# One load with a repeating source for the attention operands, and the neighbourhood bias loaded one block ahead

## The chip, the cores and the metric

The kernel runs on one core of one Trainium2 chip. The metric is the device time of one execution in microseconds, as the median of several runs. The engines are TensorE (PE, with its weight loads PEld), VectorE (DVE), ScalarE (ACT), GpSimd (POOL) and SyncE (SP). SP and POOL issue the DMAs here.

## What is computed

One inference step of a two-layer backbone, for 128 context tokens (the prompt) and 512 latent tokens, 640 columns in all, with model width 1024. Each layer normalises its input, sends it through one input projection into four parallel token mixers, merges them with sigmoid gates, projects, and adds a SwiGLU FFN:

```python
    A gated DeltaNet, bidirectional, chunked, centred short conv on q/k/v;
    B differential attention with learned lambda and 2-D axial rotary on latent tokens;
    C HGRN2 gated linear recurrence with state expansion, bidirectional, chunked;
    D 2-D neighbourhood attention (min(8,ROWS) x 16 window, relative-position bias).
```

The change concerns mixers B and D. In both, latent queries see 256 cached context keys and their own keys; in D a latent query sees a window of the 8 x 64 grid, and a relative-position bias is added to its scores, masked outside the window:

```python
        p = jax.nn.softmax(jnp.einsum('bhqmd,bhkmd->bhmqk', qi, k).astype(F32) * scale, axis=-1)
        pd = p[:, :, 0] - lam * p[:, :, 1]
```

## The kernel before

Everything is float32 in value. A product of two float32 operands is made of three float32r products, high x high, high x low and low x high (`unit`, L294), so weights and activations are split into a rounded high part on ACT (`whi`, `hh`) and a rest on VectorE and POOL (`wlo`, `hl`). Weights stream from DRAM through two raw buffers `wraw`, issued on SP.

Inside a layer, `weave` (L173) interleaves Python generators and thereby fixes the order of PE's instructions by hand. The chains are the mixers' serial parts (`mix_a`, `mix_b`, `mix_c`, `mix_d`, `prep_a`, `prep_b`), the fill is the long projections (`store_fm`, `store_tok`, `pregate`, `merge`), whose product is the PSUM tile `pu`. A chain's step names what it waits for in `yield`; the planner holds a time for each tile, for a DMA the moment of its issue plus `DLAT` = 2300 ns whatever its shape, and puts the step before the next piece of fill once that time has passed. The order of ACT, VectorE, POOL and SP comes from the tile framework's scheduler. An engine works through its queue in order, so an instruction that waits holds up what stands behind it.

Mixer D (`mix_d`, L1373) has four pairs of heads in each layer, eight turns in all, called heads below. At the start of each it loads the prompt's operands, the latent queries of block 0 (`dqt`), the latent keys (`dkd`, two tiles with high and low parts in opposite halves of the partitions) and, in `split_ctx` (L1082), the raw context keys, twice, into the upper and lower 64 partitions of the tile `dod`; ACT casts them to `dkc` and VectorE forms the rests. `dod` is also the head's output tile: it comes from a pool of four buffers, and the store `oT<-dod` of the head before returns one. Then the prompt's own attention follows (scores `pds`, exponentials `dP`, transposes, products `pdo`), then four blocks of 128 latent queries. A block loads its bias `dbias` (L1451), yields until that and the rest are there, makes the scores `pds`, adds the bias on VectorE, takes the exponentials `dPl`, transposes them (`pdt`) and multiplies by the values. `dqt` of a block is loaded while the block before is worked on; `dbias` is loaded at its own block. All of D's loads are issued on SP.

Mixer B (`mix_b`, L1160) has four heads in each layer, with rotary queries and keys prepared by `prep_b` (L1051), which writes high and low parts to the DRAM tiles `bqk`. `mix_b` loads `bqt` (queries of 128 tokens, both copies of 64 rows) and `bKd` from there, on POOL, and the context keys through the same `split_ctx`, on SP, into `bo`, with the cast `bKc`. POOL also computes a part of `wlo`.

## Time and profile before

| | us |
|---|---|
| median of 3 runs | 3498.42 (3497.09 to 3504.01) |
| the profiled execution | 3495.77 |
| its span, first to last instruction | 3493.8 |
| PE busy in it | 3366.3 |
| DVE / ACT / POOL busy | 2366.3 / 1427.7 / 544.1 |

The mean granted clock of TensorE is 0.985 of full speed. Mixer D's context keys are loaded at 668 us for its first head and at 2704 us for its last. To read the tables: a wait is idle time of an engine, put down to what ended it; the chain follows the last instruction of a stretch back to what released it; a tile's view lists what its writers and readers waited for. Matmuls overlap with their weight loads, and a busy PE is not a PE at its peak.

### The profile page before, as it was taken

What the parts mean: (1) busy time and instruction counts of PE and PEld (TensorE: products, weight loads), DVE (VectorE), ACT (ScalarE), POOL (GpSimd) and SP (SyncE); (2) the same over time, 40 slices, a digit from 0 to 9 for tenths busy, and PEclk for the clock granted to TensorE, in tenths of its full rate; (3) what the DMA queues carried; (4) which work ended last, traced back from release to release, by engine and by line L of the source; (5) the groups of instructions that cost most, each with busy time, mean ns of one, the idle gap of its engine ahead of it and who ended that gap; (6) DMA issues with size and microseconds to landing.
All of it is one profiled execution on the core that took longest, in us unless ns stands there. A gap on an engine that the chain in (4) does not pass through costs nothing.

```text
span 3493.8 us, 63676 instructions
## 1 busy us (share of the span) xinstructions
PE 3366.3 (96%) x23932; PEld 3294.3 (94%) x23932; DVE 2366.3 (68%) x5497; ACT 1427.7 (41%) x3170; POOL 544.1 (16%) x592
## 2 busy tenths in 40 slices
PE   8999999899999999999999999999999999999998
PEld 5998999899999999999999899999999999999998
DVE  7689888865667577887456797778555656644445
ACT  5344444544453353222243455445444433522222
POOL 2221112421122100000002212124122121000000
PEclk9999999999999999999999999999999999999999
DMA  6444334865453354554244433348454334322222
GB/s 218 151 151 140 120 104 136 239 177 164 121 153 120 116 173 134 153 152 128 81 123 147 132 111 116 102 127 245 141 145 125 89 103 159 108 67 78 76 78 67
DMA packets 297931, 460.16 MB, mean 132 GB/s; under 512 B 48148, under 2 KB 193172, under 8 KB 297624
## 3 DMA queue, kind: packets, MB, share of 16 engines
q1 hardware_dynamic: 286296, 423.58, 39.3%
q0 software_dynamic: 11328, 32.52, 3.1%
q8 instruction: 189, 3.10, 0.4%
q14 instruction: 118, 0.97, 0.1%
HBM read 368.42 MB, written 87.56 MB: 131 GB/s over the span
## 4 chain that ended last, share of the span: by engine, by line
PE 69%; DVE 6%; DMA 5%; issue 3%; ACT 2%; POOL 1%; SPq 0%; DVEq 0%; ACTq 0%; POOLq 0%
PE pu L152 54%; PE ptk L152 2%; PE pdv L152 1%; PE pbs L152 1%; PE pbo L152 1%; PE pW L152 1%; PE pX L152 1%; PE pdt L158 1%; PE pT L152 1%; PE pca L152 1%; PE pds L152 1%; DVE cacc L107 1%; DMA wraw<-in_wd 1%; DVE wlo L107 1%; DMA moT<-oT 1%
## 5 line engine op out<-in xcount | busy, mean ns | idle before, releaser
L152 PE MATMUL pu<-hh,whi 128*128 128x320 f32 (+1 forms) x3760 | 1195.8, 318 | 18.1 <-ACT stg L107 14.9
L152 PE MATMUL pu<-hl,whi 128*128 128x320 f32 (+1 forms) x3760 | 1166.9, 310 | 2.4 <-DVE hl L107 2.4
L152 PE MATMUL pu<-hh,wlo 128*128 128x320 f32 (+1 forms) x3760 | 1167.3, 311 | 0.0
L152 PEld LDWEIGHTS pu<-hh,whi 128*128 128x128 f32 (+1 forms) x3760 | 709.2, 189 | 22.6 <-ACT stg L107 15.4
L152 PEld LDWEIGHTS pu<-hl,whi 128*128 128x128 f32 (+1 forms) x3760 | 709.5, 189 | 4.5 <-DVE hl L107 2.6
L152 PEld LDWEIGHTS pu<-hh,wlo 128*128 128x128 f32 (+1 forms) x3760 | 708.0, 188 | 1.7
L107 ACT CAST whi<-wraw 128x1024 fp32r<-128x1024 f32 (+2 forms) x410 | 390.5, 953 | 653.6 <-PE pu L152 422.7
L107 POOL TENSOR_TENSOR wlo<-wraw,whi 128x416 fp32r<-128x416 f32 (+1 forms) x209 | 324.5, 1554 | 1757.3 <-ACT whi L107 1509.9
L107 DVE TENSOR_TENSOR wlo<-wraw,whi 128x608 fp32r<-128x608 f32 (+3 forms) x410 | 389.7, 951 | 260.6 <-ACT whi L107 256.9
L152 PE MATMUL pu<-fa,whi 128*128 128x320 f32 x1152 | 253.6, 309 | 0.0
L152 PE MATMUL pu<-mo,whi 128*128 128x320 f32 x1024 | 235.1, 317 | 5.2 <-DVE mo L107 3.5
L107 DVE SCALAR_TENSOR_TENSOR x<-pu,gn,x 128x128 f32<-128x128 f32 (+1 forms) x336 | 136.6, 436 | 88.8 <-PE pu L152 87.1
L152 PEld LDWEIGHTS pu<-fa,whi 128*128 128x128 f32 x1152 | 192.6, 188 | 0.0
L152 PE MATMUL ptk<-whi,hh 128*128 128x256 f32 x640 | 192.1, 300 | 0.0
L498 DVE CUSTOM_DVE_ANT_0 junk<-wa,cs,mod 128x256 bf16<-128x256 f32 (+1 forms) x288 | 171.7, 596 | 24.9 <-DMA wa<-in_wada 20.8
L152 PE MATMUL ptk<-wlo,hh 128*128 128x256 f32 x640 | 182.0, 284 | 3.2 <-DVE wlo L107 3.2
L152 PE MATMUL ptk<-whi,hl 128*128 128x256 f32 x640 | 181.9, 284 | 0.0
L152 PEld LDWEIGHTS pu<-mo,whi 128*128 128x128 f32 x1024 | 173.0, 191 | 7.5 <-DVE mo L107 4.8
L152 PE MATMUL pu<-fa,wlo 128*128 128x320 f32 x576 | 177.8, 309 | 0.0
L152 PE MATMUL pu<-mo,wlo 128*128 128x320 f32 x512 | 160.0, 313 | 0.0
L152 PEld LDWEIGHTS ptk<-wlo,hh 128*128 128x128 f32 x640 | 123.4, 193 | 3.4 <-DVE wlo L107 3.4
L152 PEld LDWEIGHTS ptk<-whi,hh 128*128 128x128 f32 x640 | 123.7, 193 | 0.0
(422 smaller groups left out, 6123.9 us busy)
## 6 DMA issues: line engine op xcount, KB each, us to landing
wraw<-in_win SPq DMA_DIRECT2D x151, 512.0 KB, 3.8
wa<-in_wada SPq DMA_DIRECT2D x116, 256.0 KB, 3.0
wraw<-in_wg SPq DMA_DIRECT2D x44, 512.0 KB, 3.4
wraw<-in_wu SPq DMA_DIRECT2D x44, 512.0 KB, 3.5
wraw<-in_wd SPq DMA_DIRECT2D x80, 256.0 KB, 2.6
p<-stg SPq DMA_DIRECT2D x112, 160.0 KB, 2.8
wa<-in_wada SPq DMA_DIRECT2D x128, 128.0 KB, 2.4
wraw<-in_wtok SPq DMA_DIRECT2D x32, 512.0 KB, 3.9
```

The source lines that it names most:

```text
L107: r = f(*args, **kw)
L152: r = self.nc.tensor.matmul(out, lhsT, rhs, start=start, stop=stop)
L158: r = self.nc.tensor.transpose(out, src, ident)
L498: self.nc.vector.tensor_tensor_reduce(junk, raw, cs[g], 0.5, o if k0 else self.bada[:, l, m:m + 1], ALU.mult, ALU.add, o)
```

## The change

Three things are done.

1. The operands of B's queries and of D's keys get DRAM layouts of their own. `bqk` is parted into `bq` (64 rows of four blocks of 512 floats: for each 128 tokens high and low parts side by side) and `bk`; the keys of `dqk` move to `dkk`, with 256 rows in the order in which the two tiles `dkd` take them. One load of `bqt` replaces two, and one of `dkd` replaces two (of 64 rows), that is two a head instead of four. `prep_b` stores B's queries in four pieces instead of three.
2. `twice` builds a source pattern that names the same 64 rows two times, with a step of 0 in front. With it `bqt` and the raw context keys in `split_ctx` (`dod` and `bo`) are one load of 128 rows instead of two of 64.
3. `biases(b)` loads the bias; it is called for block 0 at block 0, and for block b + 1 in block b, behind the queries of block b + 1.

The whole diff:

```diff
--- before.py
+++ after.py
@@ -92,6 +92,16 @@
         p, c = i
         n = c.start // self.w
         return self.parts[n][p, c.start - n * self.w:c.stop - n * self.w]
+
+
+def dr(ap, off, *dims):
+
+    return bass.AP(tensor=ap.tensor, offset=ap.offset + off, ap=[list(d) for d in dims])
+
+
+def twice(ap, off, *dims):
+
+    return dr(ap, off, (0, 2), *dims)
 
 
 class Timed:
@@ -324,7 +334,7 @@
                     a.mul(t[:, :c0], ps[:, :c0], f)
                     self.dma(self.pd[m][:, :c0], t[:, :c0])
                 hi, lo = self.GS("sth", HT - c0, F32R), t[:, c0:].bitcast(F32R)
-                out = self.dqk[m % 4][int(f)]
+                out = self.dqk[m % 4] if f < 1 else self.dkk[m % 4]
                 if f < 1:
                     a.mul(t[:, c0:].rearrange("p (b r c) -> p r b c", b=4, c=16), ps[:, c0:HT].rearrange("p (r b c) -> p r b c", b=4, c=16), f)
                 else:
@@ -334,7 +344,8 @@
                     if f < 1:
                         self.dma(out[i].rearrange("p (b x) -> p b x", b=4)[:, :, 16 * r.start:16 * r.stop], x.rearrange("p (b x) -> p b x", b=4))
                     else:
-                        self.dma(out[i, :, 64 * r.start:64 * r.stop], x)
+
+                        self.dma(dr(out, (0, 64)[i] * TL + 64 * r.start, ((192, 64)[i] * TL, 2), (TL, 64), (1, 64 * (r.stop - r.start))), x)
             else:
                 a.copy(t, ps[:, :HT])
                 self.dma(self.pd[m][:, j * HT:(j + 1) * HT], t)
@@ -1072,18 +1083,19 @@
             self.a.copy(hi, x)
             v.tensor_tensor(lo, x, r, ALU.subtract)
 
-            for i in range(2):
-                d = self.bqk[h][i]
-                self.dma(d[:64], r[:64, i], QB)
-                self.dma(d[192:], r[64:, i], QB)
-                self.dma(d[64:192], x[:, i], QB)
-            self.ev[('b', h)] = self.t[self.bqk[h].tensor.name]
+
+            q, d = self.bq[h], self.bk[h]
+            for b, src in enumerate((r[:64, 0], x[:64, 0], x[64:, 0], r[64:, 0])):
+                self.dma(dr(q, b * 128, (4 * TL, 64), (512, 4), (1, 128)), src.rearrange("p (t c) -> p t c", c=128), QB)
+            self.dma(d[:64], r[:64, 1], QB)
+            self.dma(d[192:], r[64:, 1], QB)
+            self.dma(d[64:192], x[:, 1], QB)
+            self.ev[('b', h)] = self.t[d.tensor.name]
 
     def split_ctx(self, kc, tmp, src):
 
         raw = tmp[:, :512]
-        self.dma(raw[:64], src)
-        self.dma(raw[64:], src)
+        self.dma(raw, twice(src, 0, (512, 64), (1, 512)))
         for m in range(2):
             o_ = slice(64 - m * 64, 128 - m * 64)
             c = raw[:, m * 256:m * 256 + 256]
@@ -1175,14 +1187,12 @@
 
             Kd, Kc = [self.SA("bKd", dt=F32R) for _ in range(2)], self.SA("bKc", dt=F32R)
             Kc = [Kc[:, 0:256], Kc[:, 256:512]]
-            dq, dk = self.bqk[h][0], self.bqk[h][1]
+            dq, dk = self.bq[h], self.bk[h]
 
             def queries(t):
 
                 x = self.SA("bqt", dt=F32R)
-                src = dq[:, t * 128 - 128:t * 128].rearrange("(b p) c -> p b c", b=4)
-                for i in range(2):
-                    self.dma(x[i * 64:i * 64 + 64].bitcast(F32).rearrange("p (b c) -> p b c", b=4), src, QM)
+                self.dma(x.bitcast(F32), twice(dq, t * 512 - 512, (4 * TL, 64), (1, 512)), QM)
                 return x
             qt = {1: queries(1)}
             for m in range(2):
@@ -1388,7 +1398,7 @@
             kd, kc = [self.SA("dkd", dt=F32R) for _ in range(2)], self.SA("dkc", dt=F32R)
             kc = [kc[:, 0:256], kc[:, 256:512]]
             od = self.S("dod")
-            dq, dk = self.dqk[hp][0], self.dqk[hp][1]
+            dq, dk = self.dqk[hp], self.dkk[hp]
 
             def queries(b):
 
@@ -1397,10 +1407,13 @@
                 for i in range(2):
                     self.dma(x[i * 64:i * 64 + 64].bitcast(F32).rearrange("p (b c) -> p b c", b=4), src, QD)
                 return x
+            def biases(b):
+                x = self.SA("dbias").rearrange("p (h k) -> p h k", h=2)[:, :, :8 * WIN[b][1]]
+                self.dma(x, self.I['nab'][l, 2 * hp:2 * hp + 2, :, BOFF[b]:BOFF[b] + 8 * WIN[b][1]].rearrange("h p k -> p h k"), QD)
+                return x
             qt = {0: queries(0)}
             for hh in range(2):
-                for i in range(2):
-                    self.dma(kd[hh][i * 64:i * 64 + 64].bitcast(F32), dk[i ^ hh, hh * 64:hh * 64 + 64], QD)
+                self.dma(kd[hh].bitcast(F32), dk[128 * hh:128 * hh + 128], QD)
             self.split_ctx(kc, od, self.I['ckd'][l, hp])
 
             yield q, pr, vf
@@ -1447,11 +1460,12 @@
                     a.copy(vo, vi)
                 else:
                     self.g.tensor_scalar(vo, vi, 1.0, None, ALU.mult)
-                bias = self.SA("dbias").rearrange("p (h k) -> p h k", h=2)[:, :, :nk]
-                self.dma(bias, self.I['nab'][l, 2 * hp:2 * hp + 2, :, BOFF[b]:BOFF[b] + nk].rearrange("h p k -> p h k"))
+                if b == 0:
+                    bias = {0: biases(0)}
                 if b < 3:
                     qt[b + 1] = queries(b + 1)
-                yield bias, qt[b], kd[1], kc[1]
+                    bias[b + 1] = biases(b + 1)
+                yield bias[b], qt[b], kd[1], kc[1]
                 Ps, rcs = [], []
                 pss = []
                 for hh in range(2):
@@ -1467,7 +1481,7 @@
                     mc, ml = self.sm("d_mc", 1), self.sm("d_ml", 1)
                     nm, ss, rc = self.sm("d_nm", 1), self.sm("d_ss", 1), self.sm("d_rc", 1)
                     v.tensor_reduce(mc, ps[:, :256], AX.X, ALU.max)
-                    v.tensor_tensor_reduce(ps[:, 256:256 + nk], ps[:, 256:256 + nk], bias[:, hh], 1.0, mc, ALU.add, ALU.max, ml)
+                    v.tensor_tensor_reduce(ps[:, 256:256 + nk], ps[:, 256:256 + nk], bias[b][:, hh], 1.0, mc, ALU.add, ALU.max, ml)
                     v.tensor_scalar(nm, ml, -1.0, None, ALU.mult)
                     P = self.SA("dPl")
                     a.activation(P[:, :256 + nk], ps[:, :256 + nk], ACT.Exp, bias=nm, accum_out=ss)
@@ -1667,8 +1681,10 @@
                 t = self.pd['qk', h] = self.dr.tile([2, 128, T], F32, tag=f"qk{h}", name=f"qk{h}")
                 self.pd[16 + h], self.pd[20 + h] = t[0], t[1]
 
-            self.dqk = [self.dr.tile([2, 2, 128, TL], F32, tag=f"dqk{h}", name=f"dqk{h}") for h in range(4)]
-            self.bqk = [self.dr.tile([2, 256, TL], F32, tag=f"bqk{h}", name=f"bqk{h}") for h in range(4)]
+            self.dqk = [self.dr.tile([2, 128, TL], F32, tag=f"dqk{h}", name=f"dqk{h}") for h in range(4)]
+            self.dkk = [self.dr.tile([256, TL], F32, tag=f"dkk{h}", name=f"dkk{h}") for h in range(4)]
+            self.bq = [self.dr.tile([64, 4 * TL], F32, tag=f"bq{h}", name=f"bq{h}") for h in range(4)]
+            self.bk = [self.dr.tile([256, TL], F32, tag=f"bk{h}", name=f"bk{h}") for h in range(4)]
             self.ad = [self.dr.tile([4, 128, T], F32, tag=f"ad{i}", name=f"ad{i}") for i in range(4)]
             self.pg = P(name="pg", bufs=3, space=PSUM)
             self.pm = P(name="pm", bufs=5, space=PSUM)
```

The planner's rules are as they were, but a block of D no longer yields to a bias that was issued at that moment, and this moves the order of PE. The place is the end of block 0 in the first head (`pdv<-cst,do` transposes the block's output, `pds` are the scores of block 1, `pbo` and `pbs` are mixer B's, `pu` is fill). Before, PE went on with twelve products `pu` after that transpose, and then:

```order
L152 MATMUL pbo<-bv,be 128x128
L152 MATMUL pbs<-bKd,bqt 128x512 x2
L152 MATMUL pbs<-bKc,bqt 128x256 x2
L152 MATMUL pu<-hh,whi 128x320
L152 MATMUL pu<-hl,whi 128x320
L152 MATMUL pu<-hh,wlo 128x320
L152 MATMUL pds<-dkc,dqt 128x256 x2
```

With the change, the scores follow the transpose at once:

```order
L168 MATMUL pdv<-cst_127,do 128x128
L162 MATMUL pds<-dkc,dqt 128x256 x2
L162 MATMUL pds<-dkd,dqt 128x256 x2
L162 MATMUL pds<-dkc,dqt 128x256 x2
L162 MATMUL pds<-dkd,dqt 128x256 x2
L162 MATMUL pu<-hh,whi 128x320
```

So the score products of block 1 stand 20 instructions earlier; block for block the same holds in all heads.

On SP, the second head of layer 1, from the store of the head before (`gt` is a store of gates, `wraw` weights). Before:

```order
L163 DMA oT_20701<-dod 128x640
L283 DMA wraw<-in_win 128x1024
L163 DMA dod<-in_ckd 64x512 x2
L163 DMA gt_93<-mth 128x320
L163 DMA dbias<-in_nab 128x2x192
L163 DMA dqt<-dqk_99 64x4x128 x2
L283 DMA wraw<-in_win 128x1024
L163 DMA gt_93<-mth 128x320 x2
L283 DMA wraw<-in_wbr 128x1024
L163 DMA dbias<-in_nab 128x2x256
L163 DMA dqt<-dqk_99 64x4x128 x2
```

With the change:

```order
L173 DMA oT_20681<-dod 128x640
L173 DMA dod<-in_ckd 128x1x512
L173 DMA gt_93<-mth 128x320
L293 DMA wraw<-in_win 128x1024
L173 DMA gt_93<-mth 128x320
L173 DMA dbias<-in_nab 128x2x192
L173 DMA dqt<-dqk_99 64x4x128 x2
L173 DMA dbias<-in_nab 128x2x256
L173 DMA gt_93<-mth 128x320
```

The two halves of `dod` are one load, written 128x1x512, and a block's bias stands behind the queries of that block, ahead of the block itself.

On VectorE, the last head of layer 1, where the prompt's two maxima `d_nm` and the rests `dkc` of the context keys stand. Before:

```order
L107 TENSOR_REDUCE d_nm<-pds 128x1
L107 TENSOR_REDUCE b_mx<-pbs 128x1 x2
L107 TENSOR_SCALAR b_nm<-b_mx 128x1
L107 TENSOR_TENSOR wlo<-wraw,whi 128x608
L107 TENSOR_TENSOR dkc<-dod,dkc 64x256 x2
L107 RECIPROCAL d_rc<-d_ss 128x1
L107 TENSOR_REDUCE d_nm<-pds 128x1
```

With the change, in the seventh head, as in the second, third, fourth and sixth:

```order
L117 TENSOR_REDUCE d_nm<-pds 128x1
L117 TENSOR_SCALAR bo<-pbo,b_rc 128x128
L117 TENSOR_TENSOR dkc<-dod,dkc 64x256 x2
L117 RECIPROCAL d_rc<-d_ss 128x1
L117 TENSOR_REDUCE d_nm<-pds 128x1
```

and in the last head:

```order
L117 TENSOR_TENSOR dkc<-dod,dkc 64x256
L117 TENSOR_SCALAR do<-pdv,d_rc 128x64 x2
L117 TENSOR_TENSOR dkc<-dod,dkc 64x256
L117 SCALAR_TENSOR_TENSOR mrg<-mth,pu 128x320 x3
L117 TENSOR_TENSOR wlo<-wraw,whi 128x608
L117 TENSOR_REDUCE d_nm<-pds 128x1
L117 RECIPROCAL d_rc<-d_ss 128x1
L117 TENSOR_REDUCE d_nm<-pds 128x1
```

In the seventh head `dkc` stays between the two `d_nm`; in the last one it now stands ahead of both.

## Rows read from the trace of the kernel before

**Rows 1.** the page: busy us (share of the span) and instructions by engine.
```profile
PE 3366.3 (96%) x23932; PEld 3294.3 (94%) x23932; DVE 2366.3 (68%) x5497; ACT 1427.7 (41%) x3170; POOL 544.1 (16%) x592
```

**Rows 2.** waits of PE, whole run: who <- whom, us in total, times, longest.
```profile
PE pdt L158 <- ACT dPl L107: 15.4, 5, 6.9
...
PE pds L158 <- ACT dP L107: 4.0, 2, 2.1
```

**Rows 3.** stretches: us, busy PE, PEld, DVE, ACT, POOL, PEclk, DMA share, GB/s.
```profile
850.00:860.00 10.00, 3.65 (x24) 3.23 (x23) 3.65 (x17) 1.99 (x8) 2.29 (x4) 0.80 0.97 251
860.00:870.00 10.00, 9.50 (x49) 9.44 (x50) 4.12 (x12) 5.66 (x15) 1.67 (x1) 0.69 0.64 193
2570.00:2580.00 10.00, 6.02 (x30) 5.27 (x29) 7.10 (x20) 6.86 (x21) 2.87 (x3) 0.83 0.53 152
2680.00:2690.00 10.00, 7.04 (x51) 6.73 (x50) 5.33 (x21) 4.81 (x14) 3.71 (x5) 1.00 0.83 261
2800.00:2900.00 100.00, 100.00 (x697) 99.24 (x696) 52.91 (x124) 37.28 (x89) 23.85 (x19) 1.00 0.30 92
```

**Rows 4.** waits from 845 to 865, then the chain from 845 to 862: start, us, what.
```profile
DVE pds L107 <- DMA dbias<-in_nab: 5.6, 1, 5.6
...
851.56 8.66 DMA dbias<-in_nab
```

**Rows 5.** the tile dbias: what its reader sat idle for (us, times).
```profile
  DMA dbias<-in_nab: 7.5, 3
```

**Rows 6.** the tile dod: its loads, idle time before its readers, landing.
```profile
L163 SPq DMA_DIRECT2D dod<-in_ckd x16: 476/588/1228, 668.2 to 2704.3; - x16
...
  DMA dod<-in_ckd: 5.7, 6
...
DMA to landing us min/median/max: 2.1/2.8/5.2
```

**Rows 7.** timeline of the last head: start, us, instruction [idle before].
```profile
2703.74 1.12 SPq L163 DMA_DIRECT2D dod<-in_ckd  x2
...
2707.18 0.71 ACT L107 CAST dkc<-dod 128x256 fp32r<-128x256 f32 x2 [1.57 <-DMA dod<-in_ckd]
...
2707.62 0.85 DVE L107 TENSOR_TENSOR dkc<-dod,dkc 64x256 fp32r<-64x256 f32 x2 [1.18 <-ACT dkc L107]
...
2708.47 0.27 DVE L107 TENSOR_REDUCE d_nm<-pds 128x1 f32<-128x128 f32 x1
...
2709.68 0.44 PE L158 MATMUL pds<-cst,dP 128*128 128x128 f32 x2 [1.81 <-ACT dP L107]
```

**Rows 8.** timeline of the third head: the same two steps.
```profile
900.46 0.37 ACT L107 ACTIVATE dP<-pds,d_nm 128x128 f32<-128x128 f32 x1 [1.30 <-DVE d_nm L107]
...
901.88 0.38 PE L158 MATMUL pds<-cst,dP 128*128 128x128 f32 x2
```

**Rows 9.** a stretch with all 16 DMA engines full (columns as in rows 3).
```profile
12.00:20.00 8.00, 4.99 (x9) 0.90 (x9) 5.37 (x13) 4.13 (x11) 0.00 (x0) 1.00 1.03 414
```

**Rows 10.** DMA from 3.0 to 4.6 us: packets by size, and a load issued there.
```profile
DMA packets 192, 0.02 MB, mean 14 GB/s; under 512 B 188, under 2 KB 188, under 8 KB 192
...
crow<-in_cond SPq DMA_DIRECT2D x3, 2.0 KB
```

**Rows 11.** the tile bo: idle time of ACT before the cast bKc.
```profile
  DMA bo<-in_ckb: 4.2, 1
```

**Rows 12.** POOL's group of bqt loads; its landing; timeline of its tightest use.
```profile
L163 POOL DMA_DIRECT2D bqt<-bqk x64 | 39.7, 625 | 6.1 <-DVE mod L498 2.3 <-PE goT L158 2.0 <-PE pdv L158 1.8
...
DMA to landing us min/median/max: 2.6/5.2/8.1
...
2798.11 1.24 POOL L163 DMA_DIRECT2D bqt<-bqk  x2
...
2808.91 0.70 PE L152 MATMUL pbs<-bKd,bqt 128*128 128x512 f32 x2
```

**Rows 13.** the tile wa from 600 to 940: idle time of VectorE for it.
```profile
  DMA wa<-in_wada: 12.5, 7
```

## The prediction

> **What bounds the kernel now.** I read the page first: TensorE is busy for 96% of the span [rows 1]. No edit here takes a matmul away, so only the time in which TensorE stands still, or runs at the lower clock, can change. Next the waits of PE: over the whole run its longest is pdt behind the ACT copy or exponential that writes dPl, 15.4 us in 5 times, and pds behind dP, 4.0 us in 2; no bqt, dqt or bKd load is in that list [rows 2]. So the query loads that the change merges hold nobody up today. Then the table of 10 us windows, to see what a stall costs: from 850 to 860 PE is busy for 3.65 us, and in the next window, at a granted clock of 0.69 (a mix of the levels 1.2 and 2.4 GHz), it does 49 matmuls where a full window does 70; a still time of 4.0 us (2570) goes with 0.83, one of 3.0 us (2680) with 1.00 [rows 3].
>
> Two chains end at such stalls, and the change touches both. The first is the bias. Around 850 SP issues two of them among other loads, VectorE stands 5.6 us until the first lands, and the chain sees the second under way from 851.6 for 8.7 us [rows 4]; PE's longest pdt wait, 6.9 us, follows; VectorE waited for a bias 3 times in the run, 7.5 us in all [rows 5]. The second is the raw context key dod, which split_ctx loads at each new head of mix_d. ACT stood before its cast waiting for that load in 6 of 8 heads, 5.7 us together [rows 6]. The last head shows what hangs on it: the store oT<-dod has freed the buffer, the two half loads are issued at 2703.7, the cast dkc runs at 2707.2, VectorE's dkc at 2707.6, only then the second d_nm, then the second dP, and PE's transpose of dP comes at 2709.7 after 1.8 us of standing still [rows 7]. The cast and the subtraction stand ahead of dP and d_nm in the queues of ACT and VectorE, though the prompt tile that dP belongs to needs no context key. In the heads where PE did not wait, its cover was small: 1.05 us in the widest, from the end of dP at 900.83 to 901.88 [rows 8].
>
> **The change, part by part.**
>
> *Bias one block ahead.* Of 32 bias loads, 24 move ahead by a block. The stall at 850 goes: 6.9 us of waiting [rows 2], and with it the lower clock of the window after, (1 - 0.69) x 10 = 3.1 us [rows 3]. Gain 10.0 us. The other two bias waits are 1.9 us together; I give nothing for them. In the new order of PE the score products of a block follow the last block at once, by the order's count some 98 matmuls from the one before where it was 118; heads of mix_d finish sooner. That is worth nothing by itself: the filling products then come later, and from 2800 to 2900 PE is full as it is [rows 3].
>
> *The context keys, one load with a repeating source.* Sixteen pairs of 64 rows (8 dod, 8 bo) become sixteen loads of 128 rows of 2 KB. SP saves one issue each, about 0.5 us. The source is now 2 x 64 x 512, with the repeat slowest, and cannot be folded into 128 rows. No load of before has that form, so I bound it. If the 256 KB are dealt to 16 engines, each moves 16 KB; at 414 GB/s for 16 full engines, 25.9 GB/s each [rows 9], that takes 0.6 us. If they are dealt by the slowest dimension, two engines move 128 KB each: 5.1 us. A half load lands in 2.8 us (median), of which its 8 KB per engine are 0.3, so 2.5 us are fixed [rows 6]. The ends are 3.1 and 7.6 us from issue, against 3.4 us from the first issue to the second half's landing today (0.5 + 2.8): from 0.3 us earlier to 4.2 us later. I take the upper end, for the nearest row: the four crow loads of 2.0 KB, whose pattern begins with one row, show in their window as the only 4 packets of 2 KB or more, where 16 engines would have had 128 bytes each [rows 10]. So a load is dealt out by the dimension it begins with, and not by bytes.
>
> The Trainium skill speaks on both sides here (DMA: Bandwidth & Descriptors, Rules for kernel authors): for two transfers to disjoint partition halves it advises one 128-partition transfer, and a line further it warns that a leading zero-stride broadcast of c copies confines the whole DMA to at most c engines. By the first the sum would be about 3485 us, by the second it is the one below; no run here shows a repeating source yet.
>
> What 4.2 us do: in the new order dkc still stands between the two d_nm of VectorE in heads 2, 3, 4, 6 and 7. There PE gets the lateness less the cover, which I take at half the widest, 0.55 us, for the four that did not wait: 5 x 4.2 - 4 x 0.55 = +18.8 us. In the first and fifth head the cast comes long after the load and nothing is felt. In the eighth the new order issues dod ahead of the store and takes the casts out of that place: its 1.8 us go. For bo, ACT waited in one head only, 4.2 us [rows 11]; there the lateness counts in full, +4.2 us, elsewhere the cast comes late enough. New stalls of about four us may bring the lower clock with them, as the one at 2570 did: (1 - 0.83) x 10 = 1.7 us [rows 3]. I take that for three of the five, since the one at 2680 brought none: +5 us.
>
> *Queries of mix_b.* 64 POOL issues of 0.62 us become 32 [rows 12], -20 us of POOL, and 48 stores of bqk become 56, at the same price +5 us. POOL is busy for 16% [rows 1], and no POOL work is among PE's long waits: zero. Each merged bqt has the same repeating source, so it may land in 5.2 + 4.2 = 9.4 us instead of 5.2. The tightest of 32 is issued at 2798.7 and used at 2808.9, 10.2 us [rows 12]; it is just covered. If that cover were gone the price would be a few tenths.
>
> *Stores and keys.* The bq stores move the same bytes in pieces of 512 B; dkd needs 16 issues of SP in place of 32. The stores of the high key parts (dkk) begin with a dimension of 2 as well, 48 or 80 KB to each of two engines, 2 to 3 us instead of under 0.5; that gives one of six gs buffers back later, at 16 places. The reader comes much later. All zero, with the rival below for the crowding.
>
> *The sum.* -10.0 + 18.8 - 1.8 + 4.2 + 5 = +16.2 us. The profiled execution took 3495.77 us (span 3493.8), 2.65 us under the median of the runs: 3495.8 + 16.2 + 2.6 = 3514.6, so **3515 us**, 0.5% slower.
>
> **The rivals.**
>
> *The merged load is dealt out to all engines* (it ends on the other side: faster). Then each context key lands 0.3 us earlier than now: -10.0 for the bias, -1.8 for the eighth head, about -1.5 for five heads: 3498.4 - 13.3 = 3485 us. For it: 128 rows in the target, which is how every load of before is dealt. Against: the crow packets. It is decided by the number of engines: the five heads and bo cost 6 x L - 2.2 us for a lateness L, and stalls like that at 2680 cost no clock, so that 11.8 us of gains are used up at L = 2.3 us, when the load itself takes 3.2 us, about three engines. On four or more the kernel is not slower. Chance 15%.
>
> *The lateness is there and mostly hidden.* If the new order's shorter blocks move dP so that only two of the five heads feel it, the terms are 8.4 + 1.7 - 11.8, about -2 us: within 0.2% (about what a measurement of this kernel can tell from no change), some 3497 us. For it: PE's order is rewritten from 745 us on, by a planner that knows no lateness. Against: ACT already arrived before the load in 6 of 8 heads. 15%.
>
> *Crowding.* Two engines held for 5.1 us by each of 16 loads on SP's queue, and again by 32 bqt, make the loads queued behind late on those two engines: wa, for which VectorE already waits 12.5 us, 7 times [rows 13], and wraw. Were 16 such loads late by half of 5.1 us, and PE to feel half, +20 us: 3535 us. For it: DMA engines at 0.97 from 850 to 860 [rows 3]. Against: whi shows no such waits among PE's longest. 10%.
>
> **How the numbers follow.** The forecast has 60%, its own range 3505 to 3528 (lateness 3.4 to 5 us, three to six heads). The four cases make: faster by over 0.2% 17% (the first rival and a thin tail of the second), within 0.2% 15%, slower 68%. The range that should hold 8 in 10 reaches from 3487, which cuts off half of the first rival, to 3538, which takes in half of the crowding.
>
> **What would show it.** Right: dod<-in_ckd and bo<-in_ckb landing at 7 to 9 us; ACT idle until dod some 25 us in 5 heads; PE pds behind dP at 20 us instead of 4.0; no wait for dbias. Wrong: landings near 3 us, or landings of 8 us with pds behind dP unchanged; a bqt or a dkd load among PE's releasers would be a place I priced at nothing.

## The result, and the profile after

The changed kernel takes **3590.0 us** (median of 4 runs, 3585.0 to 3593.1), the kernel before, run beside it, 3500.9 us (3497.1 to 3504.0): a ratio of 1.0245 [1.0231 to 1.0260], 89 us slower. The forecast was 3515 us with a range of 3487 to 3538: the right sign, and a fifth of the size.

The page of the changed kernel, its span and PE's row:

```profile
span 3590.7 us, 63529 instructions
...
PE 3401.2 (95%) x23932; PEld 3322.3 (93%) x23932; DVE 2370.8 (66%) x5497; ACT 1426.7 (40%) x3170; POOL 528.6 (15%) x568
```

Against [rows 1] PE is "busy" 34.9 us longer with the same number of matmuls. The mean granted clock of the whole run fell from 0.985 to 0.975, which is (1 - 0.975) x 3590.7 - (1 - 0.985) x 3493.8 = 37 us of full-speed work, close to the 34.9. Span less busy time rose from 127.5 to 189.5 us, by 62; with the 34.9 that is the 97 us by which the span of this execution grew. So about two thirds of the loss are PE standing still, and about one third goes with the lower clock around it (the clock is given to 0.001, which is 3.6 us).

Where it stands still, from the waits of PE over the whole run (columns as in [rows 2]):

```profile
PE pu L162 <- ACT stg L117: 23.0, 7, 9.3
PE pds L168 <- ACT dP L117: 21.6, 5, 4.9
PE pdt L168 <- ACT dPl L117: 12.6, 4, 4.8
PE pbs L162 <- DMA bpr<-qk: 11.0, 2, 5.7
...
PE pdv L168 <- ACT dvw L117: 6.7, 1, 6.7
```

PE behind dP went from 4.0 us to 21.6 [rows 2], as forecast, and its five times are the heads that were named: 2, 3, 4, 6 and 7. But the forecast list ended there. stg was 14.9 us in 2 times before, and dvw was not in the list at all. What the readers of the two context tiles sat idle for, in the views of the tiles dod and bo:

```profile
  DMA dod<-in_ckd: 46.8, 7
```

```profile
  DMA bo<-in_ckb: 29.0, 4
```

Before, these were 5.7 us in 6 heads [rows 6] and 4.2 us in one [rows 11]. The bias did what it was meant to do: no reader waits for dbias any more [rows 5]. The second head shows the forecast chain behind the load as it was drawn (timeline: start, us, instruction, idle time before it):

```profile
815.88 0.58 SPq L173 DMA_DIRECT2D dod<-in_ckd  x1
...
824.26 0.71 ACT L117 CAST dkc<-dod 128x256 fp32r<-128x256 f32 x2 [6.42 <-DMA dod<-in_ckd]
824.70 0.87 DVE L117 TENSOR_TENSOR dkc<-dod,dkc 64x256 fp32r<-64x256 f32 x2 [5.77 <-ACT dkc L117]
...
825.57 0.26 DVE L117 TENSOR_REDUCE d_nm<-pds 128x1 f32<-128x128 f32 x1
...
826.42 0.36 ACT L117 ACTIVATE dP<-pds,d_nm 128x128 f32<-128x128 f32 x1
...
826.93 0.69 PE L168 MATMUL pds<-cst,dP 128*128 128x128 f32 x2 [4.61 <-ACT dP L117]
```

The load is issued at 815.9; its cast starts 8.4 us later. VectorE's rests stand ahead of the second d_nm, and the transpose of the prompt's dP comes after 4.6 us of idle PE. The load was also issued late: the store oT<-dod of the head before went out at 806.8, 9.1 us earlier (3.0 us in the kernel before), and in between SP stood until 814.4 ahead of two loads of wa, while VectorE waited 7.5 us for the wa before them. In the packed trace the load can be told by its 128 packets of 2 KB, where no other load with such rows is under way. In five heads that allow it they start over 5.8 to 6.6 us, and the last starts 7.8 to 9.1 us after the issue. The cast bKc of mixer B does the same to a tile of mixer D, here at 889 us:

```profile
888.91 0.41 ACT L117 CAST bKc<-bo 128x256 fp32r<-128x256 f32 x1 [6.39 <-DMA bo<-in_ckb]
889.22 0.35 ACT L117 COPY dvw<-dv 128x192 f32<-128x192 f32 x1
...
889.62 0.66 PE L168 MATMUL pdv<-cst,dvw 128*96 128x128 f32 x2 [6.68 <-ACT dvw L117]
```

ACT stood 6.4 us for bo; behind it in ACT's queue was dvw of the other mixer, which PE needed: 6.7 us. And there are stalls in which no context key stands. Two waits for loads of weights, over the whole run:

```profile
DVE junk L509 <- DMA wa<-in_wada: 35.0, 19, 7.5
...
ACT whi L117 <- DMA wraw<-in_win: 22.2, 7, 5.6
```

In the kernel before they were 24.4 us in 22 times and 10.2 us in 5. At 708 us PE waits for stg, a copy that stands behind a cast of weights which ACT had waited 5.5 us to receive:

```profile
704.90 1.04 ACT L117 CAST whi<-wraw 128x1024 fp32r<-128x1024 f32 x1 [5.50 <-DMA wraw<-in_win]
```

```profile
708.61 0.63 PE L162 MATMUL pu<-hh,whi 128*128 128x320 f32 x1 [7.22 <-ACT stg L117]
```

Four of the windows with the worst stalls (columns as in [rows 3]):

```profile
700.00:710.00 10.00, 2.78 (x15) 2.51 (x14) 9.47 (x16) 3.98 (x7) 4.66 (x6) 0.83 0.63 187
810.00:820.00 10.00, 6.14 (x28) 5.72 (x27) 3.80 (x13) 0.53 (x3) 0.00 (x0) 0.66 0.32 96
820.00:830.00 10.00, 5.39 (x29) 5.13 (x27) 2.34 (x8) 4.67 (x15) 1.67 (x1) 0.81 0.23 61
880.00:890.00 10.00, 3.32 (x26) 3.04 (x24) 2.77 (x10) 3.08 (x7) 3.83 (x5) 0.88 0.59 180
```

In the second and third, PE stands still for about four of the ten us while the DMA engines, all sixteen taken together, are at 0.32 and 0.23 of their time. So it is not for want of bandwidth over all of them that the data is late.

### The profile page after: what moved, and what is told of

Same layout as the page of the kernel before. It is cut to its first block, busy times and chain, and to the rows that moved or that the text cites. A ratio compares the mean times of both kernels' runs of the same rounds, so it can differ in the third digit from the quotient of the medians.

```text
span 3590.7 us, 63529 instructions
## 1 busy us (share of the span) xinstructions
PE 3401.2 (95%) x23932; PEld 3322.3 (93%) x23932; DVE 2370.8 (66%) x5497; ACT 1426.7 (40%) x3170; POOL 528.6 (15%) x568
## 3 DMA queue, kind: packets, MB, share of 16 engines
q1 hardware_dynamic: 285336, 423.58, 38.1%
q0 software_dynamic: 25280, 32.63, 3.3%
## 5 line engine op out<-in xcount | busy, mean ns | idle before, releaser
L117 POOL TENSOR_TENSOR wlo<-wraw,whi 128x416 fp32r<-128x416 f32 (+1 forms) x209 | 315.7, 1511 | 1839.6 <-ACT whi L117 1538.9
```

The costliest lines, as they stand in the source:

```text
L117: r = f(*args, **kw)
```

## The experiments

"Before" is run again beside each group, and a ratio is to that; the changed kernel's 3590.0 us stand beside a before of 3500.9 us. Differences between groups are therefore good to a few us: the 53 us of e1 are 55 by the ratios, the 77 of e4 the same. Theory A was the prediction's: a late load, felt by its own reader. Theory B was its rival, crowding. Theory C blamed the new order of PE. D1 and D2 divide what is left between that order and the new layouts; L (lateness) and K (crowding) are A and B again, for the load of the context keys alone. Runs with the repeat as the second dimension put keys or queries into other rows of the tile and give another output; they serve for the time alone.

### Where the 89 us sit (before: 3504.9 us)

**e1_ctx_inner.**

```diff
-        self.dma(raw, twice(src, 0, (512, 64), (1, 512)))
+        self.dma(raw, dr(src, 0, (512, 64), (0, 2), (1, 512)))
```

> The changed kernel with one edit: in the load of the context keys (dod, bo) the repeat is the second dimension of the source and no longer the first; bytes, number of loads and the order of all engines stay. The keys then lie in other rows of the tile, so the attention on the context computes something else. Theory A (a load that begins with the repeat is dealt to two DMA engines, is late by some 7 us, and this lateness holds ACT and VectorE: PE behind dP +17.6 us, dvw 6.7, cZ 6.2, and the lower clock after them): most of the loss of 89 us comes back, 3525 us or less. Theory B (every transfer on two engines, stores of dkk and loads of bqt too, makes what is queued behind it on those two engines late): about half comes back, 3535 to 3555. Theory C (the new order of PE that the earlier bias brings is itself the slower one): little comes back, over 3570. In A and B ACT's wait for dod falls from 46.8 us to about 6.

Measured: 3537.0 us, 1.0088 [1.0071 to 1.0104]: 53 us back of 89, in the range of theory B, though at its fast end. ACT's idle time for dod falls from 46.8 to 12.7 us, for bo from 29.0 to 1.3, and PE's behind dP from 21.6 to 5.5. The 128 packets of a dod load now start over 1.3 to 1.7 us in three of the four heads that allow it, and over 4.0 in the fourth. The order of two dimensions in one source pattern is worth 53 us.

**e2_bqt_inner.**

```diff
-                self.dma(x.bitcast(F32), twice(dq, t * 512 - 512, (4 * TL, 64), (1, 512)), QM)
+                self.dma(x.bitcast(F32), dr(dq, t * 512 - 512, (4 * TL, 64), (0, 2), (1, 512)), QM)
```

> The changed kernel with the repeat of the bqt loads moved to the second dimension; order of all engines unchanged, mixer B's queries in other rows. Theory A: bqt is covered, no change (3585 to 3595). Theory B: bKd, rr and bpr, which stand behind bqt on POOL's queue, land earlier (bKd 12.0 us back to about 6), PE's waits for bpr of 11.0 us fall by some 6, and 3570 to 3583. Theory C: no change.

Measured: 3571.9 us, 1.0192 [1.0175 to 1.0210]: 18 us back, as theory B had it. POOL's loads show when they land. The DMA issues of the changed kernel (count, size, median us to landing), then those of this run:

```profile
bqt<-bq POOLq DMA_DIRECT2D x32, 256.0 KB, 10.3
...
bKd<-bk POOLq DMA_DIRECT2D x16, 256.0 KB, 12.0
```

```profile
bqt<-bq POOLq DMA_DIRECT2D x32, 256.0 KB, 5.0
...
bKd<-bk POOLq DMA_DIRECT2D x16, 256.0 KB, 7.1
```

The same bytes land in 10.3 us or in 5.0, and bKd, which stands behind them on POOL's queue, in 12.0 or 7.1. PE's wait for bpr, through which theory B had the gain come, did not move (11.2 us). What fell is PE's wait for stg, from 23.0 to 17.0 us, and the loss of clock (0.979 in this run against 0.975); the path from bqt to these is not shown.

**e3_dkk_fold.**

```diff
-    self.dma(dr(out, (0, 64)[i] * TL + 64 * r.start, ((192, 64)[i] * TL, 2), (TL, 64), (1, 64 * (r.stop - r.start))), x)
+    self.dma(dr(out, 128 * i * TL + 64 * r.start, (TL, 128), (1, 64 * (r.stop - r.start))), x)
```

> The changed kernel with the 16 stores of the high key parts written as 128 rows in one stretch of dkk, where the change writes them as 2 x 64 rows; PE's order unchanged, D's latent keys in other rows. Theory A: these stores cost little, 3580 to 3592. Theory B: ACT's 5.5 us for wraw at 700 us, with PE's 7.2 us behind it, VectorE's waits for wa at 660 to 740, and ACT's 11.2 us for the stores at 2380 to 2600 go, 3550 to 3572. Theory C: no change.

Measured: 3586.8 us, 1.0237 [1.0222 to 1.0252]: 3 us, inside the intervals. Theory B's guess about these stores was wrong: a target that begins with 2 costs next to nothing here. The stores of the high parts are on two engines all the same, if the count of packets under e12 is read as it is there: SP's queue has 285336 packets in the changed kernel and 285560 in this run, 14 more for each of the 16 stores of the high key parts (the two times 64 rows of the low parts follow at one step, so they make one stretch of 128).

**e4_all_inner**, the three edits above together.

> All three edits together (context keys, bqt, dkk), so that no transfer begins with a dimension of 2; same order of PE as the changed kernel. Theories A and B: the whole loss and the bias gain come out, 3485 us (3478 to 3495), below the kernel before. Theory C: the order itself is slow, 3530 or more. Between them (3500 to 3525) the earlier bias or the smaller pieces of the stores would cost something of their own.

Measured: 3512.7 us, 1.0024 [1.0011 to 1.0036]. The three add up (53 + 18 + 3 against 77), and PE's wait behind dP is back at 4.0 us. But the kernel is 8 us above before, not 20 below: the middle case of the expectation.

### The rest, part by part (before: 3505.2 us)

**e5_bias_only.**

```diff
+            def biases(b):
...
-                bias = self.SA("dbias").rearrange("p (h k) -> p h k", h=2)[:, :, :nk]
...
+                    bias[b + 1] = biases(b + 1)
```

> The kernel before with the bias edit alone; its order of PE is that of the changed kernel, row for row, its loads and layouts are those of before. The run without any transfer on two engines (e4_all_inner) was 8 us above the kernel before, where I had expected 10 to 20 below. Theory D1 (the new order of PE costs about as much as the bias stall, or more): 10 to 20 us above before. Theory D2 (the order gains, and the layouts of bq, bk and dkk with their small pieces take it back): 6 to 15 us below before. In both no reader waits for dbias.

Measured: 3508.0 us, 1.0016 [1.0004 to 1.0028]: 3 us above, between the theories. No reader waits for dbias. Two windows of this run:

```profile
850.00:860.00 10.00, 7.92 (x60) 7.59 (x60) 4.69 (x19) 5.90 (x16) 4.29 (x6) 1.00 0.57 170
970.00:980.00 10.00, 6.17 (x40) 5.76 (x39) 3.76 (x14) 3.21 (x9) 6.41 (x10) 0.92 0.80 217
```

The window that had 3.65 us of PE [rows 3] has 7.92; another one, full in the kernel before, now has 6.17: there PE waits 3.8 us for bpr, mixer B's prompt operand.

**e6_inner_no_bias**: e4_all_inner with the last edit undone.

> e4_all_inner without the bias edit: each bias loaded at its own block, so PE's order is that of the kernel before, row for row; new layouts, one load each for context keys and bqt, none that begins with a dimension of 2 (keys and queries in other rows). Theory D1: at the kernel before or up to 8 us below. Theory D2: 10 to 20 us above before. The waits for dbias of some 7.5 us are back in both.

Measured: 3509.9 us, 1.0018 [1.0005 to 1.0031]. So the new layouts by themselves cost some 5 us, the bias some 3, and neither gains. Which of the layouts' stores or loads that is was not tried further.

**e7_ctx_only**, on the kernel before.

```diff
-        self.dma(raw[:64], src)
-        self.dma(raw[64:], src)
+        self.dma(raw, twice(src, 0, (512, 64), (1, 512)))
```

> The kernel before with one edit: the context keys dod and bo by one load whose source begins with the repeat. PE's order is that of before. If the load is simply late and holds ACT and VectorE wherever it stands, 45 to 60 us above before, as e1_ctx_inner took 53 us off the changed kernel. If it is mainly the tighter blocks of the new order that expose the lateness, 10 to 30 us above before (the prediction's terms without the bias: 18.8 + 4.2 + 5 - 1.8 = 26). PE's waits behind dP at 15 us or more in both.

Measured: 3558.4 us, 1.0158 [1.0129 to 1.0186]: 53 us, the same as in the changed kernel. The new order of PE is not what exposes it; theory C is out. PE's wait behind dP is 32.3 us in 7 times in this run.

**e8_halves.**

```diff
...
-        self.dma(raw, twice(src, 0, (512, 64), (1, 512)))
+        self.dma(raw[:64], src)
+        self.dma(raw[64:], src)
...
-                self.dma(x.bitcast(F32), twice(dq, t * 512 - 512, (4 * TL, 64), (1, 512)), QM)
+                for i in range(2):
+                    self.dma(x[i * 64:i * 64 + 64].bitcast(F32), dq[:, t * 512 - 512:t * 512], QM)
```

> The changed kernel with every transfer that begins with a dimension of 2 as two of 64 rows: context keys as before, bqt as two loads from the new bq, the high keys as two stores to dkk. Values are those of the reference, PE's order that of the changed kernel. If the two engines are all that is wrong with the merged loads, it equals e4_all_inner within 5 us. If saving the second issue is worth something, it is 5 to 15 us above e4_all_inner.

Measured: 3516.3 us, 1.0042 [1.0026 to 1.0058], 4 us above e4_all_inner by the medians and 6 by the ratios, with intervals that overlap. One issue in place of two is worth a few us at most: there was little to win.

### Lateness or crowding (before: 3502.4 us)

**e9_late_two** and **e10_late_halves**: the load stays in split_ctx, the casts go into a function of their own, called behind the prompt's attention.

```diff
+            self.cast_ctx(kc, od[:, :512])
             yield o,
             self.tp(po[:, 128:256], o, self.ident)
```

> The kernel before with the context keys by one load that begins with the repeat, as in e7_ctx_only, and with mixer D's casts dkc and rests moved behind the prompt's attention, so that on VectorE they stand behind both d_nm in seven of eight heads; B's bKc stays. Theory L (the lateness itself costs, through ACT and VectorE standing before the cast): most of the 53 us of e7_ctx_only goes, 3505 to 3525. Theory K (the two engines, held for 5 us a load, make other loads late): most stays, over 3540.

> The kernel before, loads as they are (two halves), with the casts of D moved as in e9_late_two; PE's order is that of e9_late_two, so the two differ by the load alone. ACT's 5.7 us for dod and PE's 4.0 us behind dP go: 3493 to 3502. Theory L: e9_late_two is 5 to 20 us above it (bo, and heads with little cover). Theory K: 40 us or more.

Measured: 3562.5 us, 1.0173 [1.0150 to 1.0195], and 3500.3 us, 1.0002 [0.9987 to 1.0016]. By the expectation this speaks for theory K, but the trace of e9_late_two shows that the edit did not do its work. The scheduler left the cast ahead of the copy of dP on ACT, and PE waited for that copy instead (pdo behind dP, 25.6 us in 5 times):

```profile
809.36 0.71 ACT L117 CAST dkc<-dod 128x256 fp32r<-128x256 f32 x2 [5.39 <-DMA dod<-in_ckd]
...
810.23 0.36 ACT L117 COPY dP<-pds 128x256 f32<-128x256 f32 x1
```

So e9 decides nothing. e10 came out in its range, but not for the reason given: ACT still waited 7.6 us for dod, and PE 4.3 us behind dP.

**e12_extra_two** and **e13_extra_inner**: 16 loads that nobody reads, on the kernel before.

```diff
         self.dma(raw[64:], src)
+        self.dma(self.SA("scr"), twice(src, 0, (512, 64), (1, 512)))
```

(in e13 `dr(src, 0, (512, 64), (0, 2), (1, 512))`).

> The kernel before plus 16 loads that nobody reads: behind each pair of context halves the same 256 KB once more into a spare tile, with the repeat in front. PE's order is that of before. Nothing waits for them, so against e13_extra_inner this is the price of holding two engines alone. Theory K: 25 us or more above e13_extra_inner. Theory L: within 5 us. By the 18 us that e2_bqt_inner gave back over 32 loads: 9 us.

> The same 16 extra loads with the repeat as the second dimension; all engines in the order of e12_extra_two. The price of 16 more loads of 256 KB as such: 0 to 8 us above the kernel before.

Measured: 3557.0 us, 1.0156 [1.0135 to 1.0176], against 3505.3 us, 1.0007 [0.9994 to 1.0020]. Sixteen loads that **nobody reads** cost 52 us, 3.2 us each, if they begin with the repeat, and 3 us in all (inside the interval) if they do not. Theory L, by which a late load is felt by its own reader, cannot say that; crowding is real, and large. That the loads are on two engines can be counted. SP's queue in e12 and then in e13 (packets, MB, share of 16 engines):

```profile
q1 hardware_dynamic: 288376, 427.78, 38.5%
```

```profile
q1 hardware_dynamic: 288600, 427.78, 39.2%
```

The kernel before has 286296, so an extra load is 130 packets in e12 and 144 in e13. Both have the 128 rows of 2 KB; what is left is 2 packets and 16 (of 4 bytes each in the packed trace), which fits one for each engine that takes part.

Two things in these runs are not as the expectation has them. First, something does wait for the unread loads, namely SP itself (waits of SP in e12):

```profile
SPq L173 <- DMA scr<-in_ckb: 16.4, 4, 5.7
```

With the two other rows of scr it is 26.5 us in 7 times, against 3.4 us in e13. In the packed trace SP's issues use eight semaphores in turn, and a load of dkd issued at 687.1, the eighth issue behind the unread load of 674.3, has the same one and goes out when that load has landed. Second, the scheduler put the unread load of dod ahead of the context halves in six of eight heads, by 4 to 13 us, and the store oT<-dod, which must land before a buffer of dod is free, takes a median of 8.6 us in e12 and 4.4 in e13. So the halves go out later, and PE's wait behind dP, the one that the prediction had put down to lateness, is 14.9 us in e12 and 3.5 in e13.

How crowding works is also seen at the stall that the bias made in the kernel before, on SP. With the extra load dealt out (e13, start, us the issue took):

```profile
853.35 0.58 SPq L173 DMA_DIRECT2D scr<-in_ckb  x1
853.99 0.61 SPq L173 DMA_DIRECT2D dbias<-in_nab  x1
854.70 1.60 SPq L173 DMA_DIRECT2D dqt<-dqk  x2
856.47 0.61 SPq L173 DMA_DIRECT2D dbias<-in_nab  x1
```

and with it on two engines (e12):

```profile
862.70 0.57 SPq L173 DMA_DIRECT2D scr<-in_ckb  x1
863.32 0.73 SPq L173 DMA_DIRECT2D dbias<-in_nab  x1
864.15 5.94 SPq L173 DMA_DIRECT2D dqt<-dqk  x2
870.27 1.42 SPq L173 DMA_DIRECT2D dbias<-in_nab  x1
```

What stands behind the load on SP's queue is late, and SP itself is held: two issues of dqt take 5.94 us where they took 1.60, and the second bias is issued 7.6 us after the extra load instead of 3.1. The waits at that place, in e13 and then in e12:

```profile
PE pdt L168 <- ACT dPl L117: 7.8, 1, 7.8
...
DVE pds L117 <- DMA dbias<-in_nab: 6.6, 1, 6.6
```

```profile
PE pdt L168 <- ACT dPl L117: 12.1, 1, 12.1
DVE pds L117 <- DMA dbias<-in_nab: 11.1, 1, 11.1
```

Neither dbias nor dPl reads the extra load. In e12 PE is busy for 1.05 us of the ten that follow, with the DMA engines at 0.28 (columns as in [rows 3]):

```profile
870.00:880.00 10.00, 1.05 (x5) 1.05 (x6) 1.97 (x11) 1.69 (x5) 0.00 (x0) 0.50 0.28 79
```

The changed kernel shows the same on SP behind its first dod:

```profile
673.02 0.59 SPq L173 DMA_DIRECT2D dod<-in_ckd  x1
...
675.61 2.83 SPq L173 DMA_DIRECT2D p<-stg  x1
678.49 2.81 SPq L173 DMA_DIRECT2D dqk<-sth  x1
681.39 6.58 SPq L173 DMA_DIRECT2D dqk<-stg  x1
```

Three stores take 2.8, 2.8 and 6.6 us to issue. In the timelines of SP 9 issues of the changed kernel are longer than 2.5 us, 3 of e12, and none of the kernel before (longest 2.0), of e13 (1.9) or of e4_all_inner (2.2).

### What lateness adds, and which queue (before: 3504.3 us)

**e14_early_two** and **e15_early_halves**: D's context keys of the next head, loaded in block 2.

```diff
+                if b == 2 and hp < 3:
+                    raw = self.load_ctx(self.SA("dcr"), self.I['ckd'][l, hp + 1])
```

> The kernel before with D's context keys loaded two blocks ahead, in block 2 of the head before, into a tile of their own, by one load that begins with the repeat (B's too, at its place). e9_late_two left the cast ahead of the copy of dP on ACT, so lateness and crowding were still mixed there; here the load has tens of us before its cast. If the lateness costs, most of the 53 us of e7_ctx_only goes: 3505 to 3520. If the two engines make other loads late, as the 52 us between e12_extra_two and e13_extra_inner say, it stays: 3540 to 3560, and ACT's wait for the context keys of D is near zero all the same.

> The same early load as two halves, nothing on two engines; all engines in PE's order of e14_early_two. The heads' waits for dod of before (5.7 us of ACT, 4.0 us of PE) go: 3490 to 3500, at or a little below the kernel before.

Measured: 3533.3 us, 1.0082 [1.0064 to 1.0099], and 3509.7 us, 1.0022 [1.0009 to 1.0035]. ACT's wait for D's context keys in e14 is down to 11.3 us in 2 times, both in the first head of a layer, which has no head before it and still loads at its own start. About half of the price is gone; 24 us are left between the twins. Mixer B's late bo (ACT waits 10.6 us for it, 4.3 in e15), the two first heads and crowding at the new place all have a part in them, and how much each is not shown. So where the load is issued sets a good part of the price. Early halves cost 5 us on the kernel before, where I had expected a gain.

**e16_extra_two_pool** and **e17_extra_inner_pool**: the extra loads of e12 and e13 with `QM` as their queue.

> The kernel before with the 16 unread loads of e12_extra_two (repeat in front) issued on POOL's queue in place of SP's. If what stands behind such a load on its own queue is what suffers, little is left, as for the 32 bqt loads (18 us, 0.56 us each): 5 to 15 us above e17_extra_inner_pool. If the two engines are lost to all queues alike, 40 to 55 us above it.

> The same 16 unread loads on POOL's queue with the repeat as the second dimension: 0 to 10 us above the kernel before, as POOL may stand before an issue until the spare tile is free.

Measured: 3531.4 us, 1.0078 [1.0053 to 1.0103], against 3505.9 us, 1.0002 [0.9991 to 1.0013]: 25 us, between the two expectations, and about half the price on SP's queue (the four runs of e16 lie between 3523 and 3540). In the tile view of scr the landing of the same load, two engines (e16) and dealt out (e17):

```profile
DMA to landing us min/median/max: 8.9/11.1/14.5
```

```profile
DMA to landing us min/median/max: 3.0/5.2/8.5
```

The unread loads stand at other moments here than in e12, and on POOL's queue such a load comes with something more: that queue has 19776 packets in e16 and 12608 in e17, 448 more for each load (of 8 bytes each in the packed trace), and as many more for each of the 32 bqt loads of the changed kernel against e2 (25280 and 10944). What these cost is not shown, so the price on POOL's queue need not be that of the two engines alone.

### Two terms of the sum (before: 3503.7 us)

**e18_bias_old_order**: e5_bias_only with the planner told the old time.

```diff
+                self.t[bias[b].tensor.name] = self.queue(self.now, bias[b]) + DLAT
```

> The kernel before with the bias loaded one block ahead, as in the change, while the planner goes on as if it were issued at its own block: PE's order is that of before, row for row. e5_bias_only (early bias, new order) was 2.7 us above the kernel before. If the new order took the gain of the 850 stall back: 8 to 12 us below before. If the stall only moves to the next thing that is late: within 4 us of before.

Measured: 3500.5 us, 0.9989 [0.9980 to 0.9998]: 3 us gained, not 10. The windows of the old stall in this run, and ACT's wait there:

```profile
850.00:860.00 10.00, 10.00 (x72) 9.79 (x71) 5.23 (x21) 6.59 (x19) 5.78 (x8) 1.00 0.86 250
860.00:870.00 10.00, 6.97 (x41) 6.50 (x40) 4.26 (x12) 4.05 (x13) 1.68 (x1) 0.85 0.85 245
870.00:880.00 10.00, 10.00 (x49) 9.87 (x49) 5.43 (x18) 3.98 (x11) 2.35 (x3) 0.64 0.21 69
```

```profile
866.26 0.46 ACT L107 CAST mo<-moT 128x320 fp32r<-128x320 f32 x1 [5.60 <-DMA moT<-oT]
```

The stall of 850 moved to 866 and is half as long (PE misses 3.0 us of the ten, where it missed 6.4 [rows 3]): ACT stands 5.6 us for moT, the next load in SP's queue that is late, and PE lies at the lower clock afterwards (0.64) as before (0.69).

**e19_extra_half**: e12_extra_two with `(1, 256)` in place of `(1, 512)`.

> e12_extra_two with half as many bytes in each of the 16 unread loads (256 of 512 columns, repeat in front, SP's queue). If the price is the time for which two engines are held, about half of the 52 us or less remains: 10 to 30 us above before. If it is a price for each such load, whatever its size: 45 us or more.

Measured: 3527.8 us, 1.0065 [1.0052 to 1.0079], 24 us above before where e12 was 55 above its own. Half the bytes, somewhat under half the price, and half of SP's waits for scr too (12.8 us against 26.5): it goes with how long the load is under way, and not by the number of such loads.

## Why the prediction was wrong

**The mechanism was found, and priced at the wrong place.** The choice of the upper end, two engines for a load that begins with the repeat, was right: 11.1 against 5.2 us in e16 and e17, 10.3 against 5.0 in e2, so 5.3 to 5.9 us later, where I had 5.1 us on the engines in place of 0.6; and on SP the packets of a dod load start over 5.8 to 6.6 us, where they start over 1.3 to 1.7 in three of four heads of e1. The Trainium skill (DMA: Bandwidth & Descriptors, Rules for kernel authors) says the same of such a pattern, and the traces agree. The step that failed is the next one: I followed the late load to its own reader, and took what else stands on its two engines for a rival of 10% ("Were 16 such loads late by half of 5.1 us, and PE to feel half, +20 us"). Crowding is no rival but a main part of the price: sixteen loads without a reader, at nearly the same places, cost 52 us, where the rival had 20, and the 32 bqt loads, whose readers were covered, cost 18. The reading that fits the runs is that each such load on SP's queue holds two engines for some six us, and that every load, store and weight tile behind it on that queue has a share on those two and is complete only when that share is. That is argued from the late landings (oT<-dod, dbias in e12) and not followed engine by engine. SP itself stands at its issues and for the landing of the load. My sign for crowding, "DMA engines at 0.97 from 850 to 860", looked at all engines together; the windows after show PE idle with the engines at 0.23 to 0.32. The loads that the rival named, wa and wraw, were the right ones to look at: VectorE's wait for wa rose from 24.4 to 35.0 us and ACT's for wraw from 10.2 to 22.2. With the context loads alone dealt out (e1) they stay, at 36.3 and 23.1; with all three edits (e4) wraw is at 11.7 and wa at 31.6.

**Queries of mix_b, priced at zero:** 18 us. I asked whether the tightest bqt was still covered (forecast landing 9.4 us, measured 10.3), found that it was, and stopped. Its cover is not the question; what shares its engines is.

**Five heads and the eighth, +18.8 - 1.8 us:** PE behind dP rose by 17.6 us (forecast 17.0), in the five heads named, so place and size were right. But ACT stood in seven heads, not five: in the first one too, and in the eighth, where PE's 1.8 us did go, for 5.0 us. "For bo, ACT waited in one head only", +4.2 us, became four heads and 29.0 us of ACT; the part of it that can be followed to PE is the 6.7 us at 889, where another mixer's dvw stood behind the cast in ACT's queue. The second rival's sum left these 4.2 us out; with them its -1.7 us becomes +2.5, which is still within its 0.2%.

**The clock, +5 us:** about 37 us in the profiled run. I took 1.7 us for three stalls; the four windows shown above have granted clocks of 0.66 to 0.88.

**The bias, -10.0 us:** -3 in the old order (e18), +3 in the new one (e5). "The stall at 850 goes" left out the question of what is late next: moT in the one, bpr in the other. So the first rival's 3485 us was out of reach too: with every load dealt out to all engines the kernel takes 3512.7 us (e4).

**Stores, zero:** 3 us for the dkk stores (e3), inside the interval, so zero holds. The layouts as a whole cost some 5 us (e6), which I had at zero too.

By the runs: context loads 53, bqt 18, dkk 3, layouts about 5, bias about 3: 82 of 89 us, within the intervals of the parts. How the 53 divide between lateness and crowding is not settled. e14 says that about half goes with D's wait and the load's place; e12 says that such loads at nearly the same places reach 52 with no reader, part of it by way of the same wait behind dP. The two do not add; that they are late in the same microseconds is the likely reason, but it is not shown.

**No version beats the kernel before by much.** The best is e18_bias_old_order, by 0.1%.

## What to carry to other kernels

Look at the first dimension of every DMA pattern, and price a load not by when its reader gets it, but by what else must pass the engines that it holds: here sixteen unread loads cost as much as sixteen late ones. If a source must repeat, two loads of 64 rows are about as good as one of 128 dealt out (4 to 6 us apart over the whole kernel here), and both are better than one that begins with the repeat. And before a stall's length is booked as a gain, find the next thing that is late at that place: of 10 us, 3 came in.

## What the runs showed of the hardware that I had not expected

- An issue on SP can itself take 2.6 to 6.6 us behind a two-engine load or store on its queue (nine in the changed kernel); the median issue takes 0.3, the longest in the kernel before 2.0. With the unread loads on POOL's queue the price is about half (25 against 52 us for 16), and no issue of SP is above 2.2 us there.
- A load's engines can be counted on SP's queue: beside its rows it leaves 2 packets if it begins with the repeat and 16 if it does not (e12, e13). On POOL's queue it leaves 448 more if it begins with the repeat (e16, e17).
- SP's issues take eight semaphores in turn in this program, so a load that lands late stops SP at the eighth issue behind it: 26.5 us in 7 times in e12.
- The price follows place, queue and size: per load 3.2 us near the context halves on SP (3.4 against the kernel before), 1.6 on POOL's queue, 0.6 for bqt, and 1.5 against the kernel before for half the bytes on SP.
- A pattern that begins with 2 on the side of the DRAM target (the dkk stores from 128 partitions) is on two engines too, by its packets (e3), and its 16 stores cost 3 us together, inside the interval. They hold SP all the same: in e1, where they are the only two-engine transfers on SP's queue, 3 issues are above 2.5 us.
